# Where the later modulations are computed: after the projection items, or among the products of the first feed-forward input stage

## The chip, the cores and the metric

The kernel runs on one core of one Trainium2 chip. The metric is the device time of one execution in microseconds (us). Engines are named as in the profile: PE is TensorE's matmul, PEld its weight load, DVE is VectorE, ACT is ScalarE, POOL is GpSimd, SP is SyncE, whose queue issues most of the DMAs here.

## What is computed

The reference is a two-layer diffusion backbone in float32 over 1024 latent tokens of width 1024, with 256 context tokens. Layer 0 mixes tokens by bidirectional chunked gated linear attention (GLA), layer 1 by a chunked gMLP; each is followed by a SwiGLU feed-forward network (FFN) of hidden width 2816. Every sub-layer is modulated by shift, scale and gate vectors that come from the conditioning vector alone. Cut to what matters:

```python
def adaln(cond, w, b):
    m = (jax.nn.silu(cond) @ w + b)[..., None, :]
    return jnp.split(m, 6, axis=-1)
...
for i in range(DEPTH):
    sh1, sc1, g1, sh2, sc2, g2 = adaln(c, mod_w[i], mod_b[i])
    a = modulate(h, sh1, sc1)
    y = gla_mixer(a, ...) if i % 2 == 0 else gmlp_chunk_mixer(a, ...)
    h = layer_norm(ALPHA * h + g1 * y, ln_g[i, 0], ln_b[i, 0])
    f = swiglu(modulate(h, sh2, sc2), ffn_w_gate[i], ffn_w_up[i], ffn_w_down[i])
    h = layer_norm(ALPHA * h + g2 * f, ln_g[i, 1], ln_b[i, 1])
```

One of the twelve vectors of 1024 numbers is a product of the 1024 conditioning values with a 1024x1024 block of `mod_w`. None of them depends on the tokens, so all but the first two may be computed at any time before their use.

## The kernel before

**Products.** Float32 matrices are split into a rounded part and a rest (`S.copy` on ACT, then a subtraction on DVE, `sub_lo`, L149), and a product is three matmuls. The big products go through units (`run_units`): a unit covers 256 output columns in seven products of half-size matrices, and each of the seven needs an operand that is made from two raw weight tiles by additions on POOL (L487, L494) and DVE (L488, L490) and a split (ACT L623, DVE L149). Operands are made up to four products ahead. A unit of the GLA's key and query columns or of the FFN is seven times twelve matmuls of 128x128 by 128x512 (L630). Several units at the start of a stage ("leading" units, two in the GLA, three in the FFN) run their products interleaved.

**Modulation.** `ada_acc` (L186) makes one vector in eight steps: each step loads 128 rows of `mod_w` (512 KB, L194, on SP's queue) into a buffer of the pool `raw` and DVE adds its product with a column of the conditioning (L196, L197 for the first step with its bias row, then L199 seven times) to the tile `ada`. After eight steps PE sums the 128 partitions: `ada_col` with sixteen matmuls of one column for a shift or scale, `ada_row` with four of 512 columns for a gate. The pool `raw` has six buffers of 512 KB, and the raw weight tiles of all units come from it too.

**Order.** The program is written as Python generators. `background(n)` (L207) advances the list `pending` of modulations by n steps; `step()` (L504) runs after each product of a unit and advances the generator that `slow` holds, every so many products. A scheduler then orders each engine's instructions; an engine runs its own in that order. `pending` holds at first the vectors of the first FFN (`SB1`), and the gates `g1` and `g2`, four vectors and 35 steps; with `EARLY = 4` (L46ff, L673) it also holds `later`: the vectors of the gMLP (`SB2`), `g3`, of the second FFN (`SB3`) and `g4`, six vectors and 52 steps. A generator's end takes a step as well.

**Stages in time.** First x is loaded and modulated; then the GLA's six units (to about 230 us), with `among` (L777) in `slow`; the context's keys and values (to about 300); sixteen projection items (`r_item`, L1168, to about 437 us), among which the backward scan runs; `background(99)` (L1179) ends what is left in `pending`; then the forward scan (`forward`, its matmuls L911, L912, L1057 and those of L158 from `w`, `S`, `raw`; to about 600), the GLA's output (to 706), the first FFN's input (`last_block`, `ffn_units`, 706 to about 1112) and its output product, and the second layer in the same way.

**Gate rows.** `og_lhs` (L1107) loads, for a group of two or four feature blocks, all pieces `rT` of the gate `r_d` before it uses the first (pool `s` of eight buffers).

Of the kernel before, what the change touches and what calls it, by code (L numbers as in the profile page):

```python
# [15 lines left out]
P = 128  # L16
# [29 lines left out]

BG = 2

EARLY = 4

FBG = 2

# [12 lines left out]
LEADG = 2  # L65
# [21 lines left out]
def backbone(  # L87
# [9 lines left out]
    nc = tc.nc  # L97
# [19 lines left out]
    def nm(s):  # L117
        cnt[0] += 1
        return f"{s}_{cnt[0]}"
# [7 lines left out]
    def Z(shape=(P, D), dt=F32, name="z"):  # L127
        return zp.tile(list(shape), dt, tag="z", name=nm(name))

    def SS(shape=(P, 512), dt=F32, name="s"):  # L130
        return sp.tile(list(shape), dt, tag="s", name=nm(name))
# [7 lines left out]
    def PM(shape=(P, 512)):  # L139
        return pm.tile(list(shape), F32, tag="pm", name=nm("pm"))  # L140
# [4 lines left out]
    def f32(ap):  # L145
        return ap.bitcast(F32)
# [57 lines left out]
    box = {}  # L204
    pending = []

    def background(steps):  # L207

        for _ in range(steps):
            if not pending:  # L210
                return
            try:
                next(pending[0])
            except StopIteration:
                pending.pop(0)
# [23 lines left out]
    def next_cols(key, i, s, li, n_sh, n_sc):  # L239

        Sc, Bc = col_tile("S" + key), col_tile("B" + key)
        ada_col((yield from ada_acc(li, n_sh)), Bc)
        yield
        ada_col((yield from ada_acc(li, n_sc)), Sc)
        V.tensor_scalar(Sc, Sc, 1.0, None, op0=ALU.add)
        t = TT(name="lb")
        o = 48 + (i * 2 + s) * 8
        V.tensor_tensor(out=t[:, 0:NF], in0=cols1[:, o:o + 8], in1=Sc, op=ALU.mult)
        V.tensor_tensor(out=Bc, in0=Bc, in1=t[:, 0:NF], op=ALU.add)
        V.scalar_tensor_tensor(Sc, Sc, -0.5, cols1[:, 32 + o:40 + o], op0=ALU.mult, op1=ALU.mult)  # L250
        box[key] = (Sc, Bc)
        yield
# [246 lines left out]
    slow = []  # L499
# [167 lines left out]
    r_d = dr.tile([D, T], F32, name="r_d")  # L667
# [4 lines left out]
    later = [next_cols("SB2", 0, 1, 1, 0, 1), ada_row("g3", 1, 2), next_cols("SB3", 1, 0, 1, 3, 4), ada_row("g4", 1, 5)]  # L672
    pending += later[:EARLY]  # L673

# [101 lines left out]

    def among():  # L777

        for _ in range(WARM):
            background(1)  # L780
            yield
        yield from b12()
        while True:
            background(1)
            yield
# [321 lines left out]
    def og_lhs(fs, hl):  # L1107

        rs = {}
        for f in fs:  # L1110
            hl.append([Z((P, T), F32R, "ogT") for _ in range(2)])
        for half in range(2):
            for f in fs:
                rT = rs[f, half] = SS(name="rT")
                nc.sync.dma_start(rT, r_d[f * P:(f + 1) * P, half * 512:(half + 1) * 512])
        for half in range(2):
            sl = slice(half * 512, (half + 1) * 512)
            for f, h in zip(fs, hl):
                ps, rT = PM(), rs[f, half]
                for q in range(4):  # L1120
                    nc.tensor.transpose(ps[:, q * P:(q + 1) * P], OG[half * 4 + q][:, f * P:(f + 1) * P], ident)
                S.activation(rT, rT, AF.Silu)
                V.scalar_tensor_tensor(rT, ps, norm_col[:, f % 2:f % 2 + 1], rT, op0=ALU.mult, op1=ALU.mult)
                S.copy(h[0][:, sl], rT)
                V.tensor_tensor(out=h[1][:, sl], in0=rT, in1=f32(h[0][:, sl]), op=ALU.subtract)
                yield
# [9 lines left out]
    def forward():  # L1136
        stage0(0)
        for n in range(NS + 2):
# [19 lines left out]
            if n >= 2:  # L1158
# [4 lines left out]
    steps = ([ctx_step(1, 0), ctx_step(1, 1), ctx_step(0, 0), ctx_step(0, 1)]  # L1163
             + [back_step(t) for t in range(NT - 1, 0, -1)])
# [60 lines left out]
    def act_first(func, ga, xs):  # L1225

        S.activation(half(ga, 0), xs[0][0], func)
# [80 lines left out]
    def last_block(run, js, finish, units):  # L1308

        run(js, range(4), True)  # L1310
        first = finish(0)
        for n, t in enumerate(range(4, NT)):
            next(first, None)
            if n == 0:
                next(units, None)
            run(js, [t], True)
        for _ in first:
            pass
        second = finish(1)
        slow.extend([DELAY, second, GAP])  # L1320
        next(units, None)
        slow.clear()
        for _ in second:
            pass
        for _ in units:
            pass

    def residual(i, s, xn_d):

        def start(after):  # L1330
            grow = row_tile(ln_g[i, s], 1.0, after)
            brow = row_tile(ln_b[i, s], 1.0, after)
            yield
            for t in range(NT):
                acc[t] = Z(name="acc")
                queue_after(nc.sync.dma_start(acc[t], xn_d[t * P:(t + 1) * P, :]), after)
                yield
                V.scalar_tensor_tensor(acc[t], acc[t], -0.5 * ALPHA, grow, op0=ALU.mult, op1=ALU.mult)
                V.scalar_tensor_tensor(acc[t], brow, ALPHA, acc[t], op0=ALU.mult, op1=ALU.add)
        return start  # L1340
# [220 lines left out]
    norm, finish = finish_next(0, 0, "SB1", xn1, box["F"])  # L1561
# [15 lines left out]
                norm(acc[t], t)  # L1577


    def ffn_units(i, h_d, steps):  # L1580
        tiles = {}

        def gate(u):
            def first(xs):
                tiles[u] = [Z(name="gate"), Z(name="gate")]
                act_first(AF.Silu, tiles[u][0], xs)

            def rest(xs, r):
                act_rest(AF.Silu, *tiles[u], xs, r)
            return unit_col(ffn_w_gate[i], u * 256, (first, rest))  # L1590

        def up(u):
            def first(xs):
                mul(V, half(tiles[u][0], 0), xs[0][0])

            def rest(xs, r):
                mul_rest(*tiles[u], xs, r)
                store_hidden(h_d, u, *tiles[u], "ffn", u == HID // 256 - 1)
                background(steps)
            return unit_col(ffn_w_up[i], u * 256, (first, rest))  # L1600

        return run_units([k(u) for u in range(HID // 256) for k in (gate, up)], LEAD, LEAD)
# [5 lines left out]
    h0_d = dr.tile([HID // 2, 7, 512], F32, name="h0_d")  # L1608
    h1_d = dr.tile([HID // 2, 7, 512], F32, name="h1_d")
    xn2 = dr.tile([T, D], F32, name="xn2")  # L1610
# [3 lines left out]
    op = og["first"]  # L1614
    for fs in OGB[1:]:
        nxt, steps = og_ops(fs)
# [3 lines left out]
                next(steps)  # L1620
        op = nxt
    pending += later[EARLY:]
    last_block(og_run, op, finish, ffn_units(0, h0_d, FBG))
    background(99)


# [146 lines left out]
    def gm_units():  # L1773
# [2 lines left out]

    ffn_down(0, h0_d, "g2", (0, 0), xn1, lambda after: finish_next(0, 1, "SB2", xn2, after), gm_units())
    out_product(NGM // 2, gu_d, gm_w_out[0], "g3", "gm", lambda after: finish_next(1, 0, "SB3", xn3, after),
                box["p1"], residual(0, 1, xn2), ffn_units(1, h1_d, 0))
    ffn_down(1, h1_d, "g4", (1, 0), xn3, finish_out, iter(()), None)  # L1780


# [51 lines left out]
```

## Time and profile before

| | |
|---|---|
| time, median of 3 runs | 2773.28 us (2772.8 to 2778.2) |
| the profiled execution: its own time, its span | 2774.99 us, 2773.2 us |
| mean granted TensorE clock | 0.98 of 2.4 GHz |
| PE busy | 2657.5 us, 96% of the span |
| DVE, ACT, POOL busy | 1720.8, 1254.7, 672.8 us |
| bytes moved by DMA | 443.22 MB, mean 160 GB/s |
| loads of `mod_w` in units of 512 KB | 80, of 4.8 us to landing (median) |

The span is cut from the first to the last instruction. An engine is called idle only where it executes nothing; an idle engine off the path to the end costs nothing, so what counts is where PE, the engine that is busy nearly always, stands still, and who lets it go again. A matmul of 512 columns follows the one before it after about 0.227 us at full clock, though it is listed as taking 0.39, since matmuls overlap.

### The profile page before, as it was taken

The numbers are of one execution on the slowest core, as the hardware profiler recorded it, in microseconds if no ns is written. First come the engines' busy times: TensorE is split into PE (matmuls) and PEld (weight loads), VectorE is DVE, ScalarE is ACT, GpSimd is POOL, SyncE is SP. The second block draws the span as 40 slices with busy tenths as digits, with TensorE's granted clock in tenths as the row PEclk, the third lists the DMA queues.
The fourth block names the chain that finished last, engine by engine and source line by source line (L and its number), as shares of the span: only waits on it lengthen the run. The fifth ranks groups of instructions, "written<-read, shape, count | busy, mean of one in ns | idle before, by whom it ended". The sixth has DMA issues, their size and how long they took to land. (4 is left out here: it accounts for less than half of the span.)

```text
span 2773.2 us, 36002 instructions
## 1 busy us (share of the span) xinstructions
PE 2657.5 (96%) x13447; PEld 2244.6 (81%) x13447; DVE 1720.8 (62%) x2508; ACT 1254.7 (45%) x2116; POOL 672.8 (24%) x501
## 2 busy tenths in 40 slices
PE   7999995989999999999999999999999999999997
PEld 4798884777888888888899988888887888888885
DVE  6856566987844444468864355665688544444579
ACT  3533452763633333445643366664446433333442
POOL 0010010421142333210111146553201333233110
PEclk8999997999999999999999999999999999999998
DMA  6567666242232333897233255558972433235992
GB/s 239 195 208 225 200 205 220 77 146 84 77 126 88 114 107 107 242 248 220 84 123 114 92 180 175 173 176 256 267 211 77 137 107 104 83 114 185 246 272 94
DMA packets 273367, 443.22 MB, mean 160 GB/s; under 512 B 15968, under 2 KB 152050, under 8 KB 273192
## 3 DMA queue, kind: packets, MB, share of 16 engines
q1 hardware_dynamic: 245500, 389.14, 42.0%
q0 software_dynamic: 20672, 43.26, 7.9%
q10 hardware_dynamic: 7020, 8.53, 0.8%
q8 instruction: 105, 1.72, 0.3%
q14 instruction: 70, 0.57, 0.1%
HBM read 336.52 MB, written 104.35 MB: 159 GB/s over the span
## 5 line engine op out<-in xcount | busy, mean ns | idle before, releaser
L149 DVE TENSOR_TENSOR w<-raw,w 128x512 fp32r<-128x512 f32 (+2 forms) x514 | 425.8, 832 | 461.7 <-ACT w L623 324.5
L630 PE MATMUL pm<-tt,w 128*128 128x512 f32 x2160 | 522.1, 391 | 4.0 <-DVE e L555 2.6
L630 PEld LDWEIGHTS pm<-tt,w 128*128 128x128 f32 x2160 | 405.4, 188 | 92.2 <-issue 3.0
L623 ACT CAST w<-raw 128x512 fp32r<-128x512 f32 x420 | 257.7, 620 | 303.9 <-PE pm L630 97.5
L630 PE MATMUL pm<-tb,w 128*128 128x512 f32 x1440 | 353.6, 395 | 5.6 <-ACT tb L417 3.4
L630 PEld LDWEIGHTS pm<-tb,w 128*128 128x128 f32 x1440 | 271.1, 190 | 63.7 <-ACT tb L417 3.8
L1421 PE MATMUL pm<-w,w 128*128 128x512 f32 x728 | 276.5, 392 | 5.9 <-DVE e L1459 5.9
L1421 PE MATMUL pm<-w,raw 128*128 128x512 f32 x680 | 265.2, 390 | 0.0
L1421 PE MATMUL pm<-z,w 128*128 128x512 f32 x632 | 247.0, 391 | 0.7 <-DVE z L149 0.7
L487 POOL TENSOR_TENSOR raw<-raw 128x512 f32<-128x512 f32 x60 | 78.4, 1308 | 490.7 <-DVE w L149 457.8
L494 POOL TENSOR_TENSOR raw<-raw,raw 128x512 f32<-128x512 f32 (+1 forms) x68 | 103.3, 1520 | 360.6 <-DVE w L149 288.8
L630 PE MATMUL pa<-tt,w 128*128 128x512 f32 x720 | 175.2, 392 | 4.7 <-ACT tt L442 3.7
L630 PE MATMUL pa<-tb,w 128*128 128x512 f32 x720 | 173.8, 390 | 0.0
L1421 PEld LDWEIGHTS pm<-w,w 128*128 128x128 f32 x728 | 137.1, 188 | 34.5 <-issue 6.3
L1389 ACT CAST w<-raw 128x1024 fp32r<-128x1024 f32 x78 | 78.8, 1010 | 189.9 <-PE pm L1421 113.7
L630 PEld LDWEIGHTS pa<-tt,w 128*128 128x128 f32 x720 | 135.7, 189 | 34.4 <-ACT tt L442 4.5
L630 PEld LDWEIGHTS pa<-tb,w 128*128 128x128 f32 x720 | 134.8, 188 | 28.8 <-ACT w L623 0.9
L1421 PEld LDWEIGHTS pm<-w,raw 128*128 128x128 f32 x680 | 128.1, 188 | 26.6
L149 DVE TENSOR_TENSOR z<-wq,w 128x1024 fp32r<-128x1024 f32 x120 | 139.6, 1163 | 7.3 <-ACT w L1391 7.2
L1421 PEld LDWEIGHTS pm<-z,w 128*128 128x128 f32 x632 | 119.2, 189 | 26.7 <-DVE z L149 2.3
L1391 ACT CAST w<-wq 128x1024 fp32r<-128x1024 f32 x120 | 119.2, 994 | 15.4 <-PE pm L1421 7.4
L658 PE MATMUL pm<-w,tt 128*128 128x256 f32 x1008 | 124.6, 283 | 0.0
(336 smaller groups left out, 4910.4 us busy)
## 6 DMA issues: line engine op xcount, KB each, us to landing
raw<-in_mod_w_dram SPq DMA_DIRECT2D x80, 512.0 KB, 4.8
raw<-h_d SPq DMA_DIRECT2D x70, 512.0 KB, 8.1
raw<-in_gm_w_in_dram SPq DMA_DIRECT2D x48, 512.0 KB, 4.5
raw<-in_gla_w_in_dram SPq DMA_DIRECT2D x44, 512.0 KB, 7.0
raw<-in_ffn_w_gate_dram SPq DMA_DIRECT2D x44, 512.0 KB, 3.9
raw<-in_ffn_w_up_dram SPq DMA_DIRECT2D x44, 512.0 KB, 3.8
raw<-gu_d SPq DMA_DIRECT2D x42, 512.0 KB, 4.9
h_d<-gate SPq DMA_DIRECT2D x40, 512.0 KB, 3.4
```

The source lines that it names most:

```text
L149: V.tensor_tensor(out=lo, in0=src, in1=f32(hi), op=ALU.subtract)
L487: G.tensor_tensor(out=a11, in0=a11, in1=a21, op=add)
L494: G.tensor_tensor(out=a12, in0=a12, in1=a21, op=add)
L623: S.copy(op[:, 0], src)
L630: nc.tensor.matmul(ps[0], lhsT=op[:, a, kt, :], rhs=t_op(i, kt, b), start=first and kt == 0 and n == 0, stop=kt == 3 and n == 2, skip_grou ...
L658: nc.tensor.matmul(o, lhsT=t_op(i, kt, b)[:, t * P:(t + 1) * P], rhs=op[a][:, kt, :], start=first and q == 0 and kt == 0 and n == 0, stop= ...
L1389: S.copy(hi_a[:, 0:m], f32(av))
L1391: S.copy(hi_b[:, 0:m], bv)
L1421: nc.tensor.matmul(ps, lhsT=a[:, s, c], rhs=b[:, s, :], start=first and s == 0 and i == 0, stop=s == m - 1 and i == 2, skip_group_check=True)
```

## The change

`EARLY` becomes 0: the 52 steps of `later` leave the part up to `background(99)` (L1179), and `last_block` puts a generator `modulation` in `slow` once the second half of the tokens has been turned, so that a step of `later` follows every second product (`FBG = 2`) of the rest of the first FFN's input stage. (The old `background(steps)` at the end of an FFN unit found `pending` empty.) `among` lets the ten products of the leading GLA units pass without a step. `og_lhs` asks for the first two pieces of `rT` and then for one more at each piece.

```diff
--- before.py
+++ after.py
@@ -46,7 +46,7 @@
 
 BG = 2
 
-EARLY = 4
+EARLY = 0
 
 FBG = 2
 
@@ -776,6 +776,8 @@
 
     def among():
 
+        for _ in range(5 * LEADG):
+            yield
         for _ in range(WARM):
             background(1)
             yield
@@ -1109,13 +1111,20 @@
         rs = {}
         for f in fs:
             hl.append([Z((P, T), F32R, "ogT") for _ in range(2)])
-        for half in range(2):
-            for f in fs:
-                rT = rs[f, half] = SS(name="rT")
-                nc.sync.dma_start(rT, r_d[f * P:(f + 1) * P, half * 512:(half + 1) * 512])
+        todo = [(f, half) for half in range(2) for f in fs]
+
+        def load(f, half):
+            rT = rs[f, half] = SS(name="rT")
+            nc.sync.dma_start(rT, r_d[f * P:(f + 1) * P, half * 512:(half + 1) * 512])
+
+        for n in range(2):
+            load(*todo[n])
         for half in range(2):
             sl = slice(half * 512, (half + 1) * 512)
-            for f, h in zip(fs, hl):
+            for n, (f, h) in enumerate(zip(fs, hl)):
+                n += half * len(fs) + 2
+                if n < len(todo):
+                    load(*todo[n])
                 ps, rT = PM(), rs[f, half]
                 for q in range(4):
                     nc.tensor.transpose(ps[:, q * P:(q + 1) * P], OG[half * 4 + q][:, f * P:(f + 1) * P], ident)
@@ -1322,8 +1331,15 @@
         slow.clear()
         for _ in second:
             pass
+        slow.extend([0, modulation(), FBG])
         for _ in units:
             pass
+        slow.clear()
+
+    def modulation():
+        while pending:
+            background(1)
+            yield
 
     def residual(i, s, xn_d):
 
@@ -1577,7 +1593,7 @@
                 norm(acc[t], t)
 
 
-    def ffn_units(i, h_d, steps):
+    def ffn_units(i, h_d):
         tiles = {}
 
         def gate(u):
@@ -1596,7 +1612,6 @@
             def rest(xs, r):
                 mul_rest(*tiles[u], xs, r)
                 store_hidden(h_d, u, *tiles[u], "ffn", u == HID // 256 - 1)
-                background(steps)
             return unit_col(ffn_w_up[i], u * 256, (first, rest))
 
         return run_units([k(u) for u in range(HID // 256) for k in (gate, up)], LEAD, LEAD)
@@ -1620,7 +1635,7 @@
                 next(steps)
         op = nxt
     pending += later[EARLY:]
-    last_block(og_run, op, finish, ffn_units(0, h0_d, FBG))
+    last_block(og_run, op, finish, ffn_units(0, h0_d))
     background(99)
 
 
@@ -1776,7 +1791,7 @@
 
     ffn_down(0, h0_d, "g2", (0, 0), xn1, lambda after: finish_next(0, 1, "SB2", xn2, after), gm_units())
     out_product(NGM // 2, gu_d, gm_w_out[0], "g3", "gm", lambda after: finish_next(1, 0, "SB3", xn3, after),
-                box["p1"], residual(0, 1, xn2), ffn_units(1, h1_d, 0))
+                box["p1"], residual(0, 1, xn2), ffn_units(1, h1_d))
     ffn_down(1, h1_d, "g4", (1, 0), xn3, finish_out, iter(()), None)
 
 
```

What a scheduler makes of it is seen in the order of the instructions. On PE, at the end of the projection items and in the first steps of the forward scan, before (`TR` rows are the scan's cumulative sums, `ada` the modulation's sums, `w` its scores):

```order
L911 MATMUL pm_4015<-TR_2176,g_3539 128x512
L912 MATMUL pm_4015<-TR_2176,g_3539 128x512
L911 MATMUL pm_4018<-TR_2176,g_3549 128x384
L912 MATMUL pm_4018<-TR_2176,g_3549 128x384
L158 MATMUL pm_4057<-WS_2155,AS_2095 128x512
L158 MATMUL pa_3877<-cst_t,ada_3849 128x1 x8
L158 MATMUL pa_3915<-cst_t,ada_3887 128x1 x8
L158 MATMUL pa_3959<-ada_3930,cst_t 128x512
L158 MATMUL pa_3964<-ada_3930,cst_t 128x512
L158 MATMUL pa_3995<-w_3819 128x128 x2
L1057 MATMUL pa_3995<-cst_t,w_3819 128x128
```

and with the change, in the same place:

```order
L158 MATMUL pm_3725<-WS_2113,AS_2053 128x512
L913 MATMUL pm_3737<-TR_2134,g_3443 128x512
L914 MATMUL pm_3737<-TR_2134,g_3443 128x512
L913 MATMUL pm_3740<-TR_2134,g_3453 128x384
L914 MATMUL pm_3740<-TR_2134,g_3453 128x384
L158 MATMUL pa_3751<-w_3711 128x128 x2
L1059 MATMUL pa_3751<-cst_t,w_3711 128x128
```

The matmuls of three `ada` tiles, which stood between two steps of the scan, are gone from there.

On DVE, where the three leading units of the FFN's input end and the fourth begins (`w` rows are splits of operands, `raw_6711` is the fourth unit's first weight tile), before:

```order
L555 TENSOR_TENSOR e_6527<-e_6527,pm_6491 128x512
L149 TENSOR_TENSOR w_6681<-raw_6007,w_6681 128x512
L555 TENSOR_TENSOR e_6546<-e_6546,pm_6493 128x512
L149 TENSOR_TENSOR w_6696<-raw_6014,w_6696 128x512
L1231 TENSOR_TENSOR gate_6347<-u_1357_6564,pa_6495 128x512
L149 TENSOR_TENSOR w_6715<-raw_6711,w_6715 128x512
```

and with the change (the fourth unit's first tile is `raw_6494` there):

```order
L555 TENSOR_TENSOR e_6314<-e_6314,pm_6249 128x512
L199 SCALAR_TENSOR_TENSOR ada_6266<-raw_6350,cols_92,ada_6266 128x1024
L149 TENSOR_TENSOR w_6461<-raw_5763,w_6461 128x512
L199 SCALAR_TENSOR_TENSOR ada_6266<-raw_6389,cols_92,ada_6266 128x1024
L149 TENSOR_TENSOR w_6476<-raw_5770,w_6476 128x512
L199 SCALAR_TENSOR_TENSOR ada_6266<-raw_6424,cols_92,ada_6266 128x1024
L1240 TENSOR_TENSOR gate_6103<-u_1287_6332,pa_6251 128x512
L199 SCALAR_TENSOR_TENSOR ada_6266<-raw_6458,cols_92,ada_6266 128x1024
L1252 TENSOR_TENSOR u_1290_6353<-u_1290_6353,pa_6279 128x512
L199 SCALAR_TENSOR_TENSOR ada_6266<-raw_6491,cols_92,ada_6266 128x1024
L149 TENSOR_TENSOR w_6498<-raw_6494,w_6498 128x512
```

An addition of the modulation now stands between any two of the leading units' last operations on DVE, and all but one of the first vector's eight ahead of the fourth unit's first operand.

On SP's queue at the GLA's output, before (`rT` are the gate's pieces):

```order
L1569 DMA raw_5444<-in_x_dram 128x1024
L1115 DMA rT_5394<-r_d 128x512
L1115 DMA rT_5396<-r_d 128x512
L1115 DMA rT_5398<-r_d 128x512
L1115 DMA rT_5400<-r_d 128x512
L1115 DMA rT_5604<-r_d 128x512
L1115 DMA rT_5606<-r_d 128x512
L1115 DMA rT_5608<-r_d 128x512
L1569 DMA raw_5472<-in_x_dram 128x1024
L1115 DMA rT_5610<-r_d 128x512
```

and with the change:

```order
L1585 DMA raw_5198<-in_x_dram 128x1024
L1118 DMA rT_5150<-r_d 128x512
L1118 DMA rT_5152<-r_d 128x512
L1118 DMA rT_5154<-r_d 128x512
L1118 DMA rT_5203<-r_d 128x512
L1118 DMA rT_5360<-r_d 128x512
L1118 DMA rT_5362<-r_d 128x512
L1118 DMA rT_5364<-r_d 128x512
L1585 DMA raw_5228<-in_x_dram 128x1024
L1118 DMA rT_5391<-r_d 128x512
```

The rows have other buffer numbers and line numbers, and the same order.

## Rows read from the trace of the kernel before

**Rows 1.** Stretches, A:B in us: us; busy (x count) of each engine; clock; DMA share, GB/s.

```profile
75.00:107.00 32.00, 26.83 (x110) 20.59 (x109) 28.54 (x40) 12.59 (x24) 0.00 (x0) 0.89 0.57 188
110.00:250.00 140.00, 139.44 (x957) 128.37 (x956) 89.82 (x114) 57.30 (x92) 13.80 (x7) 1.00 0.64 203
438.00:478.00 40.00, 11.78 (x41) 9.15 (x41) 27.84 (x32) 1.05 (x4) 0.51 (x1) 0.54 0.80 277
480.00:595.00 115.00, 104.40 (x523) 86.45 (x522) 106.26 (x280) 78.51 (x233) 44.95 (x46) 0.99 0.21 70
770.00:1060.00 290.00, 290.00 (x1281) 240.19 (x1281) 132.37 (x191) 106.49 (x181) 99.59 (x70) 1.00 0.33 107
```

**Rows 2.** PE's waits to 520 us: who, for whom, us in all, times, longest.

```profile
PE pa L158 <- DVE ada L199: 28.4, 4, 12.2
```

**Rows 3.** Timeline of PE: start, us, instruction, [idle before and what ended it].

```profile
438.25 0.42 PE L158 MATMUL pm<-WS,AS 128*128 128x512 f32 x1
443.23 3.58 PE L158 MATMUL pa<-cst_t,ada 128*128 128x1 f32 x16 [4.57 <-DVE ada L199]
458.22 3.57 PE L158 MATMUL pa<-cst_t,ada 128*128 128x1 f32 x16 [11.42 <-DVE ada L199]
474.03 3.78 PE L158 MATMUL pa<-ada,cst_t 128*128 128x512 f32 x4 [12.23 <-DVE ada L199]
477.60 1.06 PE L158 MATMUL pa<-w 128*128 128x128 f32 x4
```

**Rows 4.** Timeline of DVE in the same stretch.

```profile
448.96 9.21 DVE L199 SCALAR_TENSOR_TENSOR ada<-raw,cols,ada 128x1024 f32<-128x1024 f32 x7
464.63 7.89 DVE L199 SCALAR_TENSOR_TENSOR ada<-raw,cols,ada 128x1024 f32<-128x1024 f32 x6
```

**Rows 5.** Timeline of PE, two vectors' sums at full clock.

```profile
250.63 1.88 PE L158 MATMUL pa<-ada,cst_t 128*128 128x512 f32 x4
278.21 1.84 PE L158 MATMUL pa<-cst_t,ada 128*128 128x1 f32 x16
```

**Rows 6.** Timelines of DVE, SP and PE around the leading GLA units.

```profile
85.47 0.75 DVE L196 TENSOR_SCALAR ada<-raw,cols 128x1024 f32<-128x1024 f32 x1
...
86.97 0.76 PE L630 MATMUL pm<-tt,w 128*128 128x512 f32 x1 [2.62 <-DVE e L555]
...
98.78 1.01 SPq L614 DMA_DIRECT2D raw<-in_gla_w_in_dram  x2
...
105.57 0.50 PE L630 MATMUL pm<-tb,w 128*128 128x512 f32 x1 [0.97 <-ACT w L623]
...
107.36 2.07 PE L630 MATMUL pm<-tb,w 128*128 128x512 f32 x4 [0.83 <-DVE w L149]
```

**Rows 7.** PE's waits from 312 to 438 us (all five make 6.0 us).

```profile
PE pa L158 <- DMA vt<-v_d: 2.5, 1, 2.5
PE pa L911 <- DVE S L980: 1.4, 1, 1.4
```

**Rows 8.** Line L199 from 110 to 250 us: ns min/median/max; idle of DVE before it.

```profile
L199 DVE SCALAR_TENSOR_TENSOR ada<-raw,cols,ada x21: 1162/1284/2701, 109.4 to 227.9; 128x1024 f32<-128x1024 f32 x21
...
  DMA raw<-in_mod_w_dram: 27.9, 14
```

**Rows 9.** DMA issues from 110 to 250 us: KB each, median us to landing.

```profile
raw<-in_mod_w_dram SPq DMA_DIRECT2D x22, 512.0 KB, 4.3
```

**Rows 10.** Groups from 770 to 1110 us: xcount | busy us, mean ns | idle before.

```profile
L149 DVE TENSOR_TENSOR w<-raw,w 128x512 fp32r<-128x512 f32 x126 | 89.5, 710 | 120.3 <-ACT w L623 119.5
L623 ACT CAST w<-raw 128x512 fp32r<-128x512 f32 x125 | 77.7, 622 | 103.8 <-PE pm L630 44.1 <-PE pa L630 19.0 <-DVE raw L490 14.0
L487 POOL TENSOR_TENSOR raw<-raw 128x512 f32<-128x512 f32 x18 | 23.2, 1290 | 102.0 <-DVE w L149 102.0
```

**Rows 11.** Timelines of SP's queue and PE where the FFN's fourth unit begins.

```profile
743.84 1.59 SPq L614 DMA_DIRECT2D raw<-in_ffn_w_up_dram  x2
...
768.45 2.88 PE L630 MATMUL pm<-tb,w 128*128 128x512 f32 x12
```

**Rows 12.** Stretches around two vectors' one-column sums (278.2, 349.8): PE, clock, DMA.

```profile
280.00:287.00 7.00, 7.00 (x57) 1.00 0.54 156
349.00:356.00 7.00, 7.00 (x38) 0.76 0.30 94
```

**Rows 13.** Timeline of PE at the GLA's output.

```profile
636.54 0.79 PE L153 MATMUL pm<-wd,ogT 128*128 128x512 f32 x1 [6.01 <-DVE acc L1199]
```

## The prediction, made before the changed kernel had run

> **What bounds the kernel now.** I first read the stretches [rows 1]: from 770 to 1060 us PE is busy for all of 290.00 us, and from 110 to 250 us for 139.44 of 140. PE is the bound, and the end can only move where PE stands still, where its clock falls, or where its own work grows. One stretch stands out: from 438 to 478 us PE is busy for 11.78 of 40 us, at a mean clock of 0.54. The chain of waits says who holds it there [rows 2]: 28.4 us in four waits of PE's sums for DVE's `ada`, line L199. The timelines show it step by step. After a scan step's matmul at 438.25 PE waits 4.57, 11.42 and 12.23 us for three vectors, sums each in 3.6 to 3.8 us, and goes on with the forward scan at 477.60 [rows 3]; DVE meanwhile adds one 128x1024 piece after the other, seven in 9.21 us and six in 7.89 [rows 4]. So `background(99)` finds DVE with some twenty steps still to do, and PE, which takes its instructions in order, stands in front of the scan until the last is done. The sums there take twice as long as elsewhere (1.84 and 1.88 us, [rows 5]) as the clock is at its lower level, 1.2 GHz, while PE idles.
>
> Three smaller places follow. In the GLA's lead the clock averages 0.89 of 2.4 GHz over 32 us and PE is busy for 26.83 [rows 1]; it waits 2.62 us for DVE's `e` (L555) just after the first modulation piece (0.75 us, L196) ran there, and later 0.97 and 0.83 us for operands whose weights SP asked for at 98.78, behind modulation loads [rows 6]. Among the projection items all waits make 6.0 us [rows 7]. And 110 to 250 us is the pattern for the new place: 22 modulation loads and 21 additions beside dense units [rows 8, 9], where DVE waits 27.9 us for the loads [rows 8] and PE still loses only 140 − 139.44 = 0.56 us.
>
> **The change, part by part.** All sums are against the profiled execution's own time, 2774.99 us.
>
> (1) *The stall before the forward scan goes.* The order shows the three `ada` tiles' sums gone from between the last item and the scan. What follows 438.25 + 0.42 then directly is what stood at 477.60: −(477.60 − 438.67) = **−38.9**. Was the scan getting ahead meanwhile, so that it would stall for DVE instead? In these 40 us DVE was busy 27.84, of which the additions are most, and ACT 1.05 and POOL 0.51 [rows 1]: the scan's preparation hardly advanced. But the scan is limited by DVE (106.26 of 115 us busy from 480 to 595, [rows 1]), so bounds are −38.9 and half of it, −19.5. I take the full value, as none of the other engines' work for the scan was done in the stall.
>
> (2) *The sums come back in another place.* The three sums that stood in the stall are now PE work in a stretch where PE has no free time: two of sixteen columns at 1.84 us and one row at 1.88, of which neighbours overlap about 0.1 each: 1.8 + 1.8 + 1.7 = **+5.3**. The other three later vectors' sums were already paid in full and only move: 0. After a column sum the clock may fall: in the 7 us after one it averaged 0.76, after another 1.00 [rows 12]. 7 × 0.24 = 1.7 us each, so two extra give 0 to 3.4; one did and one didn't, hence **+1.7**.
>
> (3) *The GLA's lead without modulation.* Out go L196's 0.75 us, of the 2.62 that PE waits (0.67 with what it overlaps), and the two waits of 0.97 and 0.83 [rows 6]. The clock: busy time of 26.83 at 0.89 loses some 32 × 0.11 = 3.5 us, of which I take half, 1.7, as the wait for `e`, of which about 2 us stay, can lower it again: 0.67 + 0.97 + 0.83 + 1.7 = **−4.2**; bounds 0, and −7.9 (2.62 + 0.97 + 0.83 + 3.5).
>
> (4) *The projection items without their fourteen steps.* The 1.4 us wait for DVE's `S` [rows 7] is behind additions; the 2.5 for `vt` is a load of the scan's own and stays. **−1.4**; bounds 0 and −4.5.
>
> (5) *The new place.* 52 steps come, one for two products of 12 matmuls, so in 104 of the stage's last 148 products (22 units of seven, less six). A product lasts 12 × 0.227 = 2.72 us, a step thus 5.44, all 283 us. DVE: 48 pieces of 1.28 us [rows 8] are 62 us onto 132.37 of 290 busy; fits. DMA: 25.2 MB in 283 us are 89 GB/s onto 107; 110 to 250 us ran at 203 [rows 1]. SP: each load stands in the queue between weight loads and its buffer is one of the six of `raw`, so a late piece can hold a unit's weights. The cover is the operands made ahead: ACT's splits wait 44.1 + 19.0 us for PE to free one [rows 10], four products or 10.9 us. From 110 to 250 us this cost 0.56 for 22 loads, here 48 / 22 × 0.56 = 1.2. The opening is worse: the order puts almost all of the first vector's eight loads ahead of the fourth unit's first tile. Eight loads are 4.19 MB, 20.7 us at 203 GB/s. The fourth unit's loads left at 743.84 and its first products began at 768.45 [rows 11]: 24.6 us of cover, just enough; I add 1.0. **+2.2**. Bounds: 0, and the nearest place where weights stood behind such loads and PE did wait, the GLA's lead: 0.97 + 0.83 idle and 1.7 of clock, 3.5 per eight loads, 48 / 8 × 3.5 = 21.
>
> (6) *Gate rows.* SP's order of the `rT` loads is the same before and after (shown above), and the 6.01 us wait at the GLA's output is for DVE's L1199 [rows 13], not for a piece: **0**, both ways.
>
> Sum: −38.9 + 5.3 + 1.7 − 4.2 − 1.4 + 2.2 = −35.3, so 2739.7 own time. The median of before lies 1.7 under its profiled execution: **2738**.
>
> **The rivals.** *The new place holds PE up (the other side).* Each of 48 loads costs PE time in the input stage, where nothing else gives way. Gains less the sums are 38.9 + 4.2 + 1.4 − 5.3 − 1.7 = 37.5, so from 37.5 / 48 = 0.78 us per load on the change is slower than before. At the price of the GLA's lead, 0.44 per load, it costs 21 instead of 2.2: 2757, still faster; at double that price, 0.9, 2779. For it: six buffers shared, one queue. Against it: 0.025 us per load from 110 to 250 us, where each buffer waited just as long. A milder form, the opening alone late by 8 to 15 us, gives 2746 to 2753.
>
> *The scan takes half back.* It now starts with DVE, ACT and POOL as little ahead as on the last item, and DVE is its bound. If half of the stall only turns into waits for DVE's chain or for `vt`, the time is 2738 + 19.5 = 2757. Against it: what DVE did in the stall was additions.
>
> *DVE and POOL block each other.* In the stretch from 110 to 250 us POOL is busy 13.80 us in all, in the FFN's input 99.59 of 290 [rows 1], so the first doesn't test it. L199 took up to 2701 ns against a median of 1284 [rows 8], 1.4 us more, about one POOL addition of 1290 [rows 10]. The 104 products are 15 units; if in each of them the two kinds of POOL additions (L487, L494) are held by one piece of 1.28 us each [rows 8], that is 15 × 2 × 1.28 = 38.4 us; if PE felt all of it, 2738 + 38.4 − 2.2 = 2774, no change. Operands are made ahead by up to four products, which hides waits of 1.3 us singly. The Trainium skill, "SBUF — State Buffer", section "Who interferes with whom", says that a vector instruction with both inputs in SBUF contends with a GpSimd instruction that reads SBUF, and that the later one blocks for the whole of the other. By that rule alone the pieces, which read two SBUF tiles, would meet POOL's additions as in this rival; the longest L199 agrees with one such meeting, no row shows PE waiting for it.
>
> *More comes back than I count.* With the lead's and the items' terms at their bounds and no clock loss after sums, 2738 − 3.7 − 3.1 − 1.7 − 1.0 = 2728.5.
>
> **How the numbers follow.** The forecast (2731 to 2745) has 0.60: its main term is read off directly. More gain, 2727 to 2731: 0.08. The new place loses 8 to 21 us, 2746 to 2757: 0.16. The scan gives half back, about 2757: 0.08. Blocking in full, about 2774: 0.03. The new place at the double price and beyond: 0.05. The range 2728 to 2754 leaves out the last two, most of the scan's case and the ends of two others, about 0.2. A difference under 0.2%, 5.5 us, is about what a measurement here cannot tell from none, so the same-time band is 2768 to 2779: faster 0.92, same 0.04 (blocking, and part of the double price), slower 0.04.
>
> **What would show it.** After the last projection item PE should go on to the scan's `w` sums with no wait for `ada`, and the clock stay at 1.00 there. The waits of 0.97 and 0.83 us in the GLA's lead are gone. Lines for the modulation's pieces stand between some 690 and 980 us, with PE busy for the full width of each stretch there. First place to look for an error: the opening of the FFN's input, where the fourth unit's first tile loads behind the modulation; then the mean of POOL's L487 and L494 against 1290 ns; then the first ten head steps of the scan, whether PE waits for DVE in them. I am wrong if PE shows idle time for weight loads or splits in the input stage of more than some 8 us, or if the scan's stretch grows by more than 5.

## The result and the profile after

The changed kernel takes 2738.45 us (median of 4, 2736.24 to 2742.3) against 2775.74 for the kernel before (median of 4, 2772.8 to 2785.37); the ratio is 0.9861, 95% interval 0.9833 to 0.9889. The forecast was 2738. The profiled execution has a span of 2736.77 us.

To see where the time came from, each stage is measured from the start of its first product to the start of the next stage's, in PE's timelines (us):

| from the start to | before | changed | lengths, difference |
|---|---|---|---|
| first context product | 247.75 | 246.23 | −1.5 |
| last scan step among the items (`pm<-WS,AS`) | 438.25 | 422.17 | 190.5, 175.9: −14.6 |
| first matmul of the forward scan (`pa<-w`) | 477.60 | 423.19 | 39.4, 1.0: −38.3 |
| first product of the GLA's output | 598.68 | 543.88 | 121.1, 120.7: −0.4 |
| first product of the first FFN | 705.95 | 649.87 | 107.3, 106.0: −1.3 |
| first FFN output product | 1130.21 | 1095.29 | 424.3, 445.4: +21.2 |
| end of the span | 2773.19 | 2736.77 | 1643.0, 1641.5: −1.5 |

Four scan matmuls (0.8 us) stand behind the scan step now and stood ahead of it before, so for like work the items give −13.8 and the stall −39.1.

Timeline of PE after the change; the second to fourth rows answer to [rows 3]:

```profile
118.66 5.49 PE L630 MATMUL pm<-tt,w 128*128 128x512 f32 x12 [4.39 <-DVE e L555]
...
422.17 0.39 PE L158 MATMUL pm<-WS,AS 128*128 128x512 f32 x1
...
423.02 0.34 PE L914 MATMUL pm<-TR,g 128*128 128x384 f32 x1
423.19 0.60 PE L158 MATMUL pa<-w 128*128 128x128 f32 x4
...
713.86 2.31 PE L158 MATMUL pa<-cst_t,ada 128*128 128x1 f32 x16 [1.32 <-DVE ada L199]
...
756.11 3.01 PE L630 MATMUL pm<-tt,w 128*128 128x512 f32 x12 [1.63 <-DVE e L555]
```

The scan follows the items without a wait. The three rows with brackets are new waits: one in the GLA, two in the FFN's input. Stretches after the change (columns as in [rows 1], with PEld second):

```profile
75.00:107.00 32.00, 30.46 (x130) 23.78 (x129) 27.52 (x41) 17.27 (x33) 4.17 (x2) 1.00 0.61 195
110.00:130.00 20.00, 15.61 (x64) 12.58 (x63) 14.70 (x18) 6.35 (x11) 4.46 (x2) 0.83 0.86 276
307.00:423.00 116.00, 112.70 (x564) 93.97 (x563) 51.50 (x94) 63.17 (x127) 18.49 (x16) 1.00 0.44 134
423.00:463.00 40.00, 38.63 (x200) 32.72 (x199) 35.09 (x100) 30.96 (x91) 13.64 (x16) 1.00 0.14 47
711.00:725.00 14.00, 12.68 (x50) 10.31 (x49) 12.81 (x14) 5.42 (x10) 7.07 (x4) 0.76 0.70 240
714.00:1004.00 290.00, 286.30 (x1266) 234.55 (x1267) 196.11 (x239) 104.08 (x180) 102.92 (x66) 0.99 0.55 180
770.00:1060.00 290.00, 287.93 (x1274) 235.89 (x1273) 178.11 (x225) 103.44 (x177) 101.42 (x67) 1.00 0.46 151
```

The GLA's lead is full now (30.46 of 32 us where it was 26.83, clock 1.00 for 0.89), but from 110 to 130 us PE has 15.61 of 20 us at 0.83: what the lead won is lost 10 us later. From 423 to 463 us, the scan's start, PE is busy for 38.63 of 40 us. From 770 to 1060 us, in the FFN's input, DVE rose from 132.37 to 178.11 us of 290, DMA from 107 to 151 GB/s, and PE lost 2.07. The stage starts 56 us earlier now, so the same part of it is 714 to 1004 us: there DVE has 196.11 us, DMA 180 GB/s, and PE lost 3.70. Around the first sum the clock averaged 0.76 over 14 us, a loss of 14 × 0.24 = 3.4. PE's waits from 645 to 1096 us (us in all, times, longest):

```profile
PE pm L630 <- DVE e L555: 3.7, 5, 1.6
PE pa L158 <- DVE ada L199: 1.3, 1, 1.3
PE pa L630 <- ACT tt L442: 0.7, 1, 0.7
PE pa L630 <- DVE tt L443: 0.2, 1, 0.2
```

No wait there is for a weight load. The last two stand in the kernel before as well; the new ones, the first two, are for DVE. Why DVE is late is in its timeline, at the GLA's wait and at the waits of 1.63 and, last, 0.44 us (PE at 837.44):

```profile
112.89 1.28 DVE L199 SCALAR_TENSOR_TENSOR ada<-raw,cols,ada 128x1024 f32<-128x1024 f32 x1
114.08 0.69 DVE L149 TENSOR_TENSOR w<-raw,w 128x512 fp32r<-128x512 f32 x1
114.80 0.69 DVE L490 TENSOR_TENSOR raw<-raw,raw 128x512 f32<-128x512 f32 x1
115.41 0.75 DVE L196 TENSOR_SCALAR ada<-raw,cols 128x1024 f32<-128x1024 f32 x1
116.19 1.21 DVE L197 TENSOR_TENSOR ada<-ada,raw 1x1024 f32<-1x1024 f32 x1
117.34 0.67 DVE L149 TENSOR_TENSOR w<-raw,w 128x512 fp32r<-128x512 f32 x1
117.94 0.67 DVE L555 TENSOR_TENSOR e<-e,pm 128x512 f32<-128x512 f32 x1
...
741.74 4.54 DVE L199 SCALAR_TENSOR_TENSOR ada<-raw,cols,ada 128x1024 f32<-128x1024 f32 x2
746.20 1.78 DVE L149 TENSOR_TENSOR w<-raw,w 128x512 fp32r<-128x512 f32 x1
747.90 1.27 DVE L199 SCALAR_TENSOR_TENSOR ada<-raw,cols,ada 128x1024 f32<-128x1024 f32 x1
749.10 0.68 DVE L149 TENSOR_TENSOR w<-raw,w 128x512 fp32r<-128x512 f32 x1
751.18 0.69 DVE L488 TENSOR_TENSOR raw<-raw,raw 128x512 f32<-128x512 f32 x1 [1.40 <-POOL raw L487]
...
755.38 0.68 DVE L555 TENSOR_TENSOR e<-e,pm 128x512 f32<-128x512 f32 x1
...
831.33 1.29 DVE L199 SCALAR_TENSOR_TENSOR ada<-raw,cols,ada 128x1024 f32<-128x1024 f32 x1 [1.25 <-DMA raw<-in_mod_w_dram]
...
835.50 1.29 DVE L199 SCALAR_TENSOR_TENSOR ada<-raw,cols,ada 128x1024 f32<-128x1024 f32 x1 [0.49 <-DMA raw<-in_mod_w_dram]
836.71 0.68 DVE L555 TENSOR_TENSOR e<-e,pm 128x512 f32<-128x512 f32 x1
```

DVE takes its instructions in order. The short addition `e` (L555), which frees an accumulator of PE's, stands behind whatever the scheduler put ahead of it: in the GLA L199, L196 and L197, 3.2 us, at 113 to 117 us. In the FFN the pieces reach it in two more ways. At 755.38 no piece stands directly ahead of it, but the operand that does was begun late: POOL's L487 waited for the L149 at 749.10, behind three pieces, and DVE stood still 1.40 us for L487 with `e` in its queue. And at 831.33 and 835.50 DVE stands still 1.25 and 0.49 us for the pieces' own loads; PE then waits 0.44 for `e`. From 645 to 1096 us DVE stood still 12.6 us, 13 times, for modulation loads, and in four of the five waits for `e` it did so (0.19 to 1.74 us) within the 6 us ahead of `e`. The ten lead products pass without a step in the program's text, yet pieces run beside them.

### The profile page after: what moved, and what is told of

It is laid out like the page before. It is cut to its first block, busy times and chain, and to the rows that moved or that the text cites. A ratio compares the mean times of both kernels' runs of the same rounds, so it can differ in the third digit from the quotient of the medians.

```text
span 2736.8 us, 35989 instructions
## 1 busy us (share of the span) xinstructions
PE 2649.6 (97%) x13447; PEld 2238.1 (82%) x13447; DVE 1732.3 (63%) x2508; ACT 1253.0 (46%) x2116; POOL 688.6 (25%) x501
## 5 line engine op out<-in xcount | busy, mean ns | idle before, releaser
L149 DVE TENSOR_TENSOR w<-raw,w 128x512 fp32r<-128x512 f32 (+2 forms) x514 | 433.5, 848 | 439.0 <-ACT w L623 271.1
L494 POOL TENSOR_TENSOR raw<-raw,raw 128x512 f32<-128x512 f32 (+1 forms) x68 | 111.7, 1644 | 370.8 <-DVE w L149 298.1
L487 POOL TENSOR_TENSOR raw<-raw 128x512 f32<-128x512 f32 x60 | 79.7, 1329 | 470.5 <-DVE w L149 437.7
L630 PE MATMUL pa<-tt,w 128*128 128x512 f32 x720 | 175.9, 394 | 4.7 <-ACT tt L442 3.7
L149 DVE TENSOR_TENSOR z<-wq,w 128x1024 fp32r<-128x1024 f32 x120 | 139.6, 1163 | 7.7 <-ACT w L1407 7.6
```

The lines of the kernel that those rows point to most:

```text
L149: V.tensor_tensor(out=lo, in0=src, in1=f32(hi), op=ALU.subtract)
L487: G.tensor_tensor(out=a11, in0=a11, in1=a21, op=add)
L494: G.tensor_tensor(out=a12, in0=a12, in1=a21, op=add)
L630: nc.tensor.matmul(ps[0], lhsT=op[:, a, kt, :], rhs=t_op(i, kt, b), start=first and kt == 0 and n == 0, stop=kt == 3 and n == 2, skip_grou ...
```

## The experiments

"Stage" is the FFN's input as in the table above; PE's waits and the clock's loss in it are sums of the idle gaps and of (1 − clock) × time. These three are of the one execution that was profiled; for e_g2spread it took 2733.65 us, 5.9 over the median:

| kernel | median us | ratio to before, interval | stage us | waits | clock |
|---|---|---|---|---|---|
| before | 2775.74 | | 424.3 | 0.9 | 0 |
| changed | 2738.45 | 0.9861, 0.9833 to 0.9889 | 445.4 | 5.9 | 3.4 |
| e_none | 2717.54 | 0.9793, 0.9777 to 0.9809 | 424.3 | 1.0 | 0 |
| e_loads | 2728.57 | 0.9833, 0.9818 to 0.9848 | 435.2 | 0.9 | 0 |
| e_gate | 2738.65 | 0.9875, 0.986 to 0.9889 | 448.3 | 7.7 | 5.1 |
| e_noskip | 2739.94 | 0.9875, 0.986 to 0.989 | 446.8 | 9.0 | 1.7 |
| e_late | 2738.79 | 0.9871, 0.9856 to 0.9886 | 444.6 | 6.8 | 1.7 |
| e_pos | 2751.21 | 0.9908, 0.9883 to 0.9934 | 455.6 | 14.5 | 5.1 |
| e_fbg1 | 2756.67 | 0.9934, 0.9917 to 0.995 | 462.5 | 19.3 | 8.5 |
| e_stall | 2752.67 | 0.9921, 0.9906 to 0.9936 | 447.8 | 12.6 | 5.1 |
| e_stall_late | 2746.87 | 0.9898, 0.9884 to 0.9913 | 439.2 | 6.2 | 1.7 |
| e_spread | 2735.96 | 0.9861, 0.9844 to 0.9877 | 435.1 | 4.2 | 1.7 |
| e_g2 | 2740.90 | 0.988, 0.9865 to 0.9895 | 454.9 | 13.0 | 5.1 |
| e_g2spread | 2727.74 | 0.9838, 0.9823 to 0.9853 | 435.4 | 4.0 | 0 |

**What the new place costs.** e_none puts other vectors' results in place of the six:

```diff
-    pending += later[EARLY:]
+    box["SB2"] = box["SB3"] = box["SB1"]
+    box["g3"] = box["g4"] = box["g2"]
```

> The changed kernel without the six later vectors: the second layer and the second FFN use the first FFN's shift, scale and gate instead, so 48 loads, 48 additions and six sums are left out. Theory (the FFN's input stage pays 21 us for them: 10.9 for six sums, 4.7 opening, 3.3 waits for e, 2 in small pieces): 2715 to 2720 us. Rival (the prediction's 14.6 for the same): 2723 to 2725. If the later stages gain by the absence too, below 2714.

2717.54 us, and the stage 424.3, that of before to 0.1 us: the new place costs 21 in all, and what follows the stage takes as long as in the changed kernel (1641.6 and 1641.5 us). e_loads keeps loads and sums and drops 42 additions (`noadd` is filled before the FFN):

```diff
-            else:
+            elif not noadd:
                 V.scalar_tensor_tensor(acc, raw, sc, acc, op0=ALU.mult, op1=ALU.add)
```

> The changed kernel with 42 of the six later vectors' additions left out (only the first of eight pieces is used); all 48 loads and the six sums stay, so the vectors are not the reference's. Theory (PE's waits for e in the FFN's input come from additions that stand ahead of e on DVE): these waits go, the sums stay, 2717.5 + 10.9 = 2728 to 2731 us. Rival (the loads, on SP's queue and in the six buffers, hold the operands): 2735 to 2739, and waits for w or raw appear.

2728.57 us, as the theory had it. PE's waits in its stage, 645 to 1112 us:

```profile
PE pa L631 <- ACT tt L443: 0.7, 1, 0.7
PE pa L631 <- DVE tt L444: 0.2, 1, 0.2
```

Those two stand in the kernel before as well. So 48 loads of 512 KB on SP's queue cost PE nothing as long as almost no addition waits for them; six sums cost 435.15 − 424.26 = 10.9, 1.8 each; and the 42 additions bring the other 445.42 − 435.15 = 10.3, of which 5.0 are waits and 3.4 clock. With the additions go their own time on DVE, DVE's standing still for their loads, the holding of a buffer until its addition is done, and their meetings with POOL; the run does not tell these apart.

**Density and place.** e_fbg1 doubles the rate:

```diff
-FBG = 2
+FBG = 1
```

> The changed kernel with a step after every product of the FFN's input instead of every second. Theory (each burst of additions ahead of an e holds PE, and denser steps make bigger bursts: 512 KB per 2.72 us beside the weights, as in the GLA's lead where 4.4 us of wait and 3.4 of clock came at this density): 2743 to 2755 us. Rival (the buffers and DVE keep up, the same steps are only over sooner): 2736 to 2740.

2756.67 us, a little past the theory's range. PE's waits in its stage:

```profile
PE pa L158 <- DVE ada L199: 8.5, 5, 5.6
PE pm L630 <- DVE w L149: 4.3, 1, 4.3
PE pm L630 <- ACT w L623: 2.4, 2, 1.3
PE pm L630 <- DVE e L555: 2.4, 1, 2.4
```

The same 48 pieces cost 462.45 − 435.15 = 27.3 in place of 10.3. Here PE waits for the vectors and splits too. DVE stood still for modulation loads for only 0.3 us of this stage, so the price here is not that of late loads. e_late begins after the leading units:

```diff
     def modulation():
+        for _ in range(8):
+            yield
         while pending:
```

> The changed kernel with the FFN's first modulation step sixteen products later, after the three leading units. Theory (the opening costs 1.32 us of wait for the eighth piece and 3.4 of clock behind it, both only because the first vector meets the change from leading to single units): 2733 to 2735 us, no wait of PE for ada. Rival (the first column sum lowers the clock wherever it stands, and a wait for the last piece goes with it): 2737 to 2739.

No wait for `ada` is left, but 5.9 us of waits for `e` have come, with this the longest:

```profile
729.97 2.42 PE L630 MATMUL pm<-tt,w 128*128 128x512 f32 x6 [2.23 <-DVE e L555]
```

2738.79 us: the rival's number, though not its mechanism. The opening is no special price; the loss takes another form. e_pos steps only after a unit's sixth, seventh and first product (`FBG` is 1, so that each product is counted):

```diff
-FBG = 2
+FBG = 1
@@ modulation
+        n = 0
         while pending:
-            background(1)
+            if n >= 15 and (n - 15) % 7 in (5, 6, 0):
+                background(1)
+            n += 1
             yield
```

> The changed kernel with the FFN's steps from the fourth unit on and only after a unit's sixth, seventh and first product, three per unit, so away from the fifth product that is followed by e. Theory (the waits for e come from pieces that stand just ahead of it): waits for e under 2 us in all, 2732 to 2735 us. Rival (the scheduler moves the pieces ahead again, or the bursts of three are as bad): 2737 to 2742.

2751.21 us (2739.08 to 2755.17), well worse: seven waits for `e`, 13.5 us. Bursts of three at this place hurt more than an even row. The pieces did not stay away from `e`: one to two of them stand within the 6 us ahead of each of the seven, and DVE stood still 37.3 us in the stage for their loads, 27 times. At the wait of 2.45:

```profile
972.10 1.28 DVE L199 SCALAR_TENSOR_TENSOR ada<-raw,cols,ada 128x1024 f32<-128x1024 f32 x1 [2.50 <-DMA raw<-in_mod_w_dram]
...
977.75 0.68 DVE L555 TENSOR_TENSOR e<-e,pm 128x512 f32<-128x512 f32 x1
```

**The stall by itself.** e_stall leaves the rest of the change out: EARLY is 4, the lead isn't passed, and only the flush goes.

```diff
             next(fwd)
-    background(99)
```

> The changed kernel with EARLY = 4, no pass over the lead's ten products, and only the flush after the projection items gone: the 28 steps that stood behind that flush go among the FFN input's products, the other 24 later steps stay in the GLA stage. Theory (the stall of 40 us goes whole; what the FFN takes costs three sums of 1.8, an opening of 4.7 and a part of the short waits for e, about 12 in all): 2743 to 2748 us, some 6 above the changed kernel, because the waits and clock drops among the items stay. Rival 1 (moving steps out of the items is neutral): 2737 to 2740. Rival 2 (the scan gives half of the stall back as waits): 2760 or more.

2752.67 us, above the theory's range and under rival 2's. The scan follows the items without a wait here too (434.82 us), so the stall does go whole; it starts 11.6 us later than in the changed kernel, as the steps among the items are still there. But the opening of the FFN loses 14 us to two waits and the clock; on DVE the second half of the tokens is turned ahead of the split that PE waits for:

```profile
698.47 4.27 PE L630 MATMUL pm<-tt,w 128*128 128x512 f32 x10 [6.45 <-DVE w L149]
705.13 3.31 PE L158 MATMUL pa<-ada,cst_t 128*128 128x512 f32 x4 [2.39 <-DVE ada L199]
```

e_stall_late adds the eight yields of e_late:

> e_stall (28 steps after the scan instead of 52) with the FFN's first step sixteen products later. Theory (e_stall lost 13.9 us at the opening alone, in 6.45 + 2.39 us of waits and 5.1 of clock, since its steps put weight splits behind the turning of the second half on DVE; the rest of its 28 steps costs what it costs elsewhere): 2740 to 2743 us, still 2 to 4 above the changed kernel, for the waits among the items that stay. Rival (the stretch is full and the loss only moves): 2750 to 2754.

Those two waits are gone and the stage falls from 447.8 to 439.2, but `e` waits 5.2 us; 2746.87 (2743.38 to 2748.71) lies between theory and rival. So removing the flush, without the rest of the change, gives 22 to 27 us of the 37 (against 2774.92 and 2774.25 of before in these runs); most of the rest is from the items.

**The pass and the gate rows.** e_noskip takes the pass of ten products out of `among`:

> The changed kernel without the pass over the ten lead products. Theory (the pass only moves the lead's wait from 84 to 114 us, 9.5 us of waits and clock before, 8.6 after): 2737 to 2741 us. Rival (the prediction's step 3, the pass is worth 4.2): 2742 to 2744.

2739.94 us: the pass is worth nothing that can be told. e_gate asks for the gate's pieces as before:

> The changed kernel with the gate's pieces asked for as before, all of a group at once. Theory (the order of SP's loads is the same either way, so nothing changes): 2736 to 2741 us, and the wait at the GLA's output stays at 5.8 to 6.0 us. Rival (the pieces asked for later free buffers or queue for others): over 5 us slower, with the wait at the GLA's output longer.

2738.65, nothing. The wait at the GLA's output was 6.45 us for the changed kernel's 5.82, outside the 5.8 to 6.0 that I had expected. Its order of loads is the changed kernel's, yet its stage is 2.9 us longer, with waits for the same things at other sizes: so much differs between executions, and smaller differences between stages in the table say nothing.

**Two ways on.** e_spread gives the FFN one step for five products, and the second FFN's vectors (SB3, g4) go to the gMLP's first units, one for a product (cut; what is left of them is ended ahead of the stage's first mixing):

```diff
-FBG = 2
+FBG = 5
-    pending += later[EARLY:]
+    pending += later[:2]
+    del later[:2]
@@ out_product, ahead of its last loop over units
+        if later:
+            pending.extend(later)
+            later.clear()
+            slow.extend([0, modulation(), 1])
```

> The changed kernel with only the gMLP's shift, scale and gate (26 steps) in the first FFN's input stage, one for five products, and the second FFN's (26 steps) one for each product of the gMLP's first units, which last longer. Theory (PE's loss beside the sums comes from additions that pile up on DVE ahead of e; at this spacing they don't): the six sums of 10.9 us stay, waits for e and ada together under 2 us, 2728 to 2732 us. Rival (each piece costs PE some 0.2 us wherever it stands): 2736 to 2739.

The stage does fall to 435.1, but with three sums in it, not six, and 3.3 us of waits for `e` are left; the gMLP's first units take 263.8 us for 255.7, of which some 5.5 are the three sums. 2735.96: the rival's price is nearer. No piece stands within the 6 us ahead of those two `e` now, so it is not that additions pile up. At the longer wait, 2.11 us, DVE stood still 4.92 us for one piece's load, the operand behind that piece was begun late, and `e` stands behind the operand:

```profile
917.63 1.28 DVE L199 SCALAR_TENSOR_TENSOR ada<-raw,cols,ada 128x1024 f32<-128x1024 f32 x1 [4.92 <-DMA raw<-in_mod_w_dram]
...
925.14 0.68 DVE L555 TENSOR_TENSOR e<-e,pm 128x512 f32<-128x512 f32 x1
```

DVE stood still 24.4 us for such loads here, against 12.6 in the changed kernel. e_g2 moves g2's nine steps too, starts the FFN's sixteen products later as e_late does, and the GLA's later (only the last is shown):

```diff
-        for _ in range(5 * LEADG):
+        for _ in range(5 * LEADG + 9):
-WARM = 12
+WARM = 3
```

> The changed kernel with the first FFN's gate g2 also in the FFN's input stage (61 steps, from the sixteenth product on) and the GLA's first steps later, three instead of twelve before the second half's operands. Theory (the wait of 4.4 us for e at 114 and the 3.4 of clock after it come from the GLA's first modulation pieces): both go, the eight pieces cost 2 more in the FFN, 2730 to 2734 us. Rival (that wait is the lead's own or moves on again): 2737 to 2742.

The GLA's wait goes as the theory said (first context product at 237.09 for 246.23 us; 1.8 of it is a sum that moved), but the stage grows by 9.5 to 454.9, with 12.2 us of waits for `e`. 2740.90: less the sum of 1.8, the stage grew by 7.7 us, four times the 2 that I gave the eight pieces. e_g2spread has e_g2's GLA stage and e_spread's two places, with one step for four products in the FFN from its start:

> e_g2's GLA stage with e_spread's spacing: g2 and the gMLP's vectors (35 steps) one for four products of the FFN's input, the second FFN's in the gMLP's first units. Theory (both gains add, 8 for the lead's wait and clock, 8 to 10 for the waits in the FFN): 2720 to 2726 us, near the 2717.5 of no later vectors with their sums added and the lead's loss taken off. Rival (what one place loses less the other loses more): 2730 to 2737.

2727.74 us, beside e_gate's 2738.65 on the same chip: 10.9 faster than the changed kernel's order, if 2 above the theory's range. Stretches of its GLA lead, FFN input and gMLP:

```profile
75.00:140.00 65.00, 61.76 (x277) 49.90 (x276) 40.18 (x57) 29.65 (x52) 9.06 (x5) 1.00 0.39 126
650.00:1080.00 430.00, 426.02 (x1898) 350.15 (x1897) 276.44 (x348) 172.81 (x295) 137.55 (x93) 1.00 0.42 141
1295.00:1558.00 263.00, 255.84 (x2082) 252.55 (x2081) 171.33 (x215) 112.06 (x166) 30.25 (x14) 0.99 0.46 153
```

The clock stays up in both stretches where the changed kernel loses it, and three places share the work. It differs from the changed kernel in three things at once, so which of them gives how much is not shown.

## Why the prediction was right, and where its terms were not

The time was right, and its largest term. Three smaller terms were wrong by +4.5, −8.7 and +6.4 us, and they and the rest cancelled to 1.1: that the time came out within 1 us is luck.

| term of the sum | forecast | measured | from |
|---|---|---|---|
| (1) stall | −38.9 | −39.1 | table above |
| (2) three sums more | +5.3 | +5.4 | 10.9 in the FFN, less one row (1.8) before the context and two columns (3.7) after it |
| (3) GLA's lead | −4.2 | +0.3 | −1.5, less the row's sum |
| (4) items | −1.4 | −10.1 | −13.8, less the columns' 3.7 |
| (2, 5) clock after sums, new place | +3.9 | +10.3 | 445.42 − 435.15 |
| (6) gate rows | 0 | 0 | e_gate |
| all else | 0 | −3.2 | −0.4 − 1.3 − 1.5 |
| sum | −35.3 | −36.4 | |

**(1)** held: the scan gave nothing back (−0.4 over its length), so the rival of the scan falls, and e_stall shows the same without the rest of the change.

**(3)** failed as a mechanism. I counted the waits that would go and not where the pieces would go: the lead did gain, and the next `e` paid 4.39 us and 20 × 0.17 = 3.4 of clock. e_noskip shows the pass to be worth nothing; in e_g2, where the pieces start later, the wait and the loss of clock are gone. The two waits of 0.97 and 0.83 did go, as forecast.

**(4)** was the largest error, and outside its bounds of 0 and −4.5. I read only PE's idle time among the items, 6.0 us [rows 7], and not its clock beside it. One fall of the clock there is in [rows 12], from 349 to 356 us: (2) used it as a price for the new place, and nothing took it off here. Two stretches of the kernel before show what I passed over:

```profile
262.00:269.00 7.00, 5.48 (x33) 5.49 (x34) 4.81 (x5) 1.65 (x3) 0.00 (x0) 0.76 0.90 299
312.00:438.00 126.00, 120.52 (x586) 99.50 (x587) 71.64 (x113) 64.89 (x129) 20.32 (x16) 0.97 0.55 174
```

They lose 7 × 0.24 + 126 × 0.03 = 5.5 us, and from 307 to 423 us after the change the clock is 1.00. With 3.5 us fewer waits (9.4 before, 5.9 after, from the first context product to the last scan step) that is 9.0 of 10.1; the rest I can't place.

**(5)** had the right bounds (0 to 21) and the wrong value and cause. Its price came from the stretch from 110 to 250 us, where no `e` was late; its suspect, loads that hold up the weights, cost nothing (e_loads), and its cover of four products is one for operands; `e` is not made ahead. What costs is DVE's order: `e` behind the additions, and the additions behind their loads. The rival of the new place had the side right and the way wrong: each piece costs 10.3 / 48 = 0.21 us, about half of its 0.44 and far from the 0.78 at which the gain is gone. It isn't a constant either: at twice the density it is 27.3 / 48 = 0.57, and there is still a gain.

**DVE and POOL.** This rival was there, far below its price of 38.4 us. Where POOL ran, pieces took longer: POOL in the changed kernel ahead of the wait of 1.63,

```profile
741.34 1.62 POOL L1272 TENSOR_TENSOR gate<-gate,gate 128x512 f32<-128x512 f32 x1
743.04 2.15 POOL L1274 TENSOR_TENSOR hs<-gate 128x512 f32<-128x512 f32 x1
745.27 2.16 POOL L1275 TENSOR_TENSOR hs<-gate,hs 128x512 f32<-128x512 f32 x1
749.85 1.29 POOL L487 TENSOR_TENSOR raw<-raw 128x512 f32<-128x512 f32 x1 [2.42 <-DVE w L149]
```

while two L199 took 4.54 us for 2 × 1.28, and L149 1.78 for 0.69: 3.1 us later than alone; from the L149 at 749.10 behind them runs the way by L487 to the `e` for which PE waited 1.63. The groups from 690 to 1010 us, first of the changed kernel (xcount | busy, mean ns | idle before),

```profile
L199 DVE SCALAR_TENSOR_TENSOR ada<-raw,cols,ada 128x1024 f32<-128x1024 f32 x42 | 61.2, 1458 | 12.7 <-DMA raw<-in_mod_w_dram 12.6
L494 POOL TENSOR_TENSOR raw<-raw,raw 128x512 f32<-128x512 f32 x15 | 25.1, 1676 | 49.4 <-DVE w L149 42.3 <-DVE SSB L245 7.1
```

then of e_none:

```profile
L494 POOL TENSOR_TENSOR raw<-raw,raw 128x512 f32<-128x512 f32 x16 | 20.7, 1293 | 45.0 <-DVE w L149 45.0
```

Both sides slow down: L494 by 383 ns on average, and L199, whose median stays at 1284, to a mean of 1458 and a longest of 2318. The Trainium skill ("SBUF — State Buffer", "Who interferes with whom") says that a vector instruction with two inputs in SBUF contends with a GpSimd instruction that reads SBUF; these rows agree. How much of the 10.3 us is from this and how much from the pieces' own length or the wait for their loads stays open: no run took POOL's work away, and none kept this density with every load landed early.

## What to carry to other kernels

Work that holds a queue in front of PE is worth moving into a stage that PE fills: the 39 us were safe because they could be read off directly. What it costs in the new place is set by what stands behind it on its engine's queue, here a 0.7 us addition that frees an accumulator, and by whether its own load has landed when its turn comes, for DVE, in order, stood still until it had; the engine's free share and the DMA's don't tell it. An even row cost less than bursts, and one step for two products less than one for one; thinner still left waits behind late loads. The best order found also spread the work over three stages. And when a stage's waits are summed, its clock belongs in the sum.

## What the hardware showed that I had not expected

A wait of 1.3 us, with a sum of sixteen one-column matmuls behind it, was followed by the lower clock: 3.4 us lost in the 14 us from 711 us, more than the wait itself. Two overlapping additions on DVE and POOL slow both: 2.27 us for L199's 1.28, and 1.68 on average for L494's 1.29. And 48 loads of 512 KB, in a stage that already moved 107 GB/s, cost PE nothing in e_loads; what cost was that DVE, in order, had to add them up and at times to stand still for one (4.92 us in e_spread).
